# A matmul with batch normalisation: the weight blocks loaded by one GpSimd transfer each instead of four

## The chip, the cores and the metric

The kernel runs on one core of one Trainium2 chip. The metric is the device time of one execution in microseconds (us), without any profiler; before the change it is 207.76 us, the median of three runs (207.47 to 208.3). A profile is one separate execution of the same program, recorded by the hardware profiler. Engines are named as in the profile: PE multiplies matrices (PEld is its weight load), DVE and ACT are the vector and the scalar engine, POOL is GpSimd, SP is the engine that here only starts transfers. A core has 16 DMA engines, which carry out every transfer, whichever engine issues it.

## What is computed

```python
def reference(x, weight, gamma, beta, eps):     # x (16, 512, 1024), weight (1024, 768), float32
    y = np.matmul(x, weight)                    # (16, 512, 768)
    mean = np.mean(y, axis=(0, 1), keepdims=True)
    var = np.var(y, axis=(0, 1), keepdims=True)
    y_norm = (y - mean) / np.sqrt(var + eps)
    return (gamma * y_norm + beta).astype(np.float32)
```

The 16 x 512 rows are one long dimension of 8192. Every output column needs its mean and variance over all 8192 rows before its first value can be stored.

## The kernel before

**Tiling.** The 8192 rows are worked through in 16 chunks of 512 (`C`, `CH`); the first two chunks are loaded in halves of 256 rows (`QR`). The 768 output columns are six blocks of 128. The 1024 input columns (`k`) are the contracted dimension. They lie on the 128 partitions in an unusual order, which lets DVE transpose x in blocks of 32: `k = 256 i + 64 jw + 2 c + e`, with `i` from 0 to 3, `c` from 0 to 31, and the partition is `32 i + c`. What is left on each partition are four blocks `jw` with two neighbours `e` each. A product over all of k is thus eight matmuls (`jw`, `e`) that add up in PSUM.

**The weight.** `w_sb` holds it as bf16, `[128, 4 (jw), 2 (e), 768]`. Block `jw` of it is read from four separate pieces of DRAM, one for each `i`: 32 lots of two neighbouring rows, which lie one behind another (32 x 2 x 768 x 4 bytes = 197 KB), and the four pieces start 256 rows apart. The transfers are GpSimd's and turn float32 into bf16 on the way, so that 786 KB are read and 393 KB are written for a block. `load_w(jw, jw1)` (L378) issues one transfer for each `i`, to 32 partitions; it is called for block 0, for block 1, and for blocks 2 and 3 together, so there are 12 weight transfers.

**x.** `load_x` (L386) loads some rows with four GpSimd transfers in the same manner, one for each `i`, each to 32 partitions, into a piece of the buffer `ring`; 256 rows are 1.05 MB read and 0.52 MB written. DVE transposes what came (`turn_x`, L421 or L414) into `xT_sb`. For the first two pieces the transpose is in two halves, blocks 0 and 1 and then 2 and 3.

**How the first microseconds run.** The loads are put in the order (L426): x piece 0, w block 0, x piece 1, w block 1, w blocks 2 and 3, then the other x pieces. On PE come, in this order (L754 to 771):

- `wake(8)`, matmuls on a constant tile (L574, and 22 small ones, L577), whose result is not used;
- `part(0, 1, [0])`: x piece 0 times w block 0;
- `wake(2)` (`FILL`), the same unused work again;
- `part(1, 2, [0])`: x piece 1 times w block 0;
- `part(0, 2, [1])`: both pieces times w block 1;
- then the first chunk times w blocks 2 and 3, and after that chunk by chunk.

Products of the first two column blocks are `rows_unit` (L493, x is the stationary side), those of the other four are `col_unit` (L558).

**Who sets the order.** Nothing is issued as the Python text has it. Each piece of work is a `Task` with a due time (`prio`), a cost for each engine that may do it, and what it depends on. `arrange()` runs through them in modelled time and writes out a fixed order for every engine; `seq()` holds the engines to it. Transfers are modelled by `Wires`: a task's cost on its queue is the time that issuing takes, its `dma` the time on the wires, and `count` the number of its transfers. A queue has eight places for transfers under way (`LANES = 8`), and so it is in the program too: a ninth GpSimd transfer isn't issued before the first has landed, a tenth before the second has, and so on. The planner's figures for a weight task are L436 to 438:

```python
took = 4 * 192 * 4 * (n1[0] - n) / 4 * PER_KB * 1.024
w_ready[n] = task(t, {"POOL": (2.0, 2.0)}, load_w(n, *n1), dma=took)
w_ready[n].count = 4
```

`make_identity` is a small GpSimd task of its own (`idt`), due after the last weight block and put wherever GpSimd has room.

**After the loads.** Column sums and squares are gathered while the chunks go by (L642 to L698), then columns are normalised and stored, block by block, under the matmuls of the later blocks. The last block ends with the statistics, a normalisation by DVE (L1280), transposes by PE (L1028), copies by ACT (L1293) and the stores.

Of the kernel before, what the change touches and what calls it, by code (L numbers as in the profile page):

```python
# [227 lines left out]
def kernel(  # L228
# [9 lines left out]
    nc = tc.nc  # L238
# [52 lines left out]
    def seq(bi):  # L291

        ins = bi.ins
        prev = last.get(ins.engine)
        if prev is not None:
            tc.add_manual_dep(
                ins, prev,
                mybir.DependencyInfo(mybir.DependencyClass.NoSync, mybir.DependencyReason.DATA),
                reason="order",
            )  # L300
        last[ins.engine] = ins.name
        return bi
# [48 lines left out]
    def task(prio, engines, emit, deps=(), lock=False, **kw):  # L351
        t = Task(prio, engines, emit, deps, **kw)
        t.lock = lock
        tasks.append(t)
        return t

    def dve(occ):
        return {"DVE": (occ, occ + 0.09)}

    def act(occ):  # L360
        return {"ACT": (occ, occ + 0.11)}
# [14 lines left out]
    w_ready, x_ready, x_slot, plain, last_loads = {}, {}, {}, {}, []  # L376

    def load_w(jw, jw1):  # L378
        def emit(eng):
            rows = weight.rearrange("(i jw c e) n -> i c jw (e n)", i=4, jw=JW, e=2)  # L380
            dst = w_sb.rearrange("p jw e n -> p jw (e n)")
            for i in range(4):
                seq(nc.gpsimd.dma_start(dst[32 * i:32 * i + 32, jw:jw1], rows[i, :, jw:jw1]))
        return emit

    def load_x(m0, rows, slot):  # L386
        def emit(eng):
            x_bf = piece(slot).bitcast(bf16).rearrange("p (t k) -> p t k", k=KQ)
            slot.tile = x_bf
            src = x_flat[m0:m0 + rows].rearrange("(t r) k -> r t k", r=32)  # L390
            for i in range(4):
                bi = seq(nc.gpsimd.dma_start(x_bf[32 * i:32 * i + 32], src[:, :, KQ * i:KQ * (i + 1)]))  # L392
            slot.loader.ins = bi.ins
        return emit
# [8 lines left out]
    def turn_x(xslot, slot, m0, t0, jw0, jw1, new, rows=QR):  # L403
        def emit(eng):
            single = m0 // CH in SINGLE
            if new:
                xT_sb = xtpool.tile([P, JW, 2, CH] if single else [P, JW, CH, 2], bf16, tag="xT")
                slot.tile = xT_sb
            half, row = divmod((m0 + 32 * t0) % CH, QR)
            if single:  # L410
                src = xslot.tile[:, t0:t0 + rows // 32].rearrange("p t (jw c e) -> p t jw e c", jw=JW, e=2)
                dst = slot.tile[:, :, :, half * QR + row:half * QR + row + rows]
                dst = dst.rearrange("p jw e (t r) -> p t jw e r", r=32)
                seq(nc.vector.transpose(dst[:, :, jw0:jw1], src[:, :, jw0:jw1]))  # L414
                return
            src = xslot.tile[:, t0:t0 + rows // 32].rearrange("p t k -> p (t k)").bitcast(f32)
            src = src.rearrange("p (t jw c) -> p t jw c", jw=JW, c=32)
            dst = slot.tile.rearrange("p jw m e -> p (jw m e)").bitcast(f32)
            dst = dst.rearrange("p (jw q t r) -> p q t jw r", jw=JW, q=QPC, r=32)
            dst = dst[:, half, row // 32:(row + rows) // 32, jw0:jw1]  # L420
            seq(nc.vector.transpose(dst, src[:, :, jw0:jw1]))  # L421
        return emit
# [9 lines left out]
    t = 1.0  # L432
    affine = None
    for kind, n, *n1 in order:
        if kind == "w":
            took = 4 * 192 * 4 * (n1[0] - n) / 4 * PER_KB * 1.024  # L436
            w_ready[n] = task(t, {"POOL": (2.0, 2.0)}, load_w(n, *n1), dma=took)
            w_ready[n].count = 4
            t += 2.1 * (n1[0] - n)
            if n1[0] == JW:  # L440
                idt = task(t, {"POOL": (0.6, 0.6)}, lambda eng: make_identity(nc, ident))
                task(t, act(0.25), lambda eng: seq(nc.scalar.copy(ident32, ident)), [idt])
            continue
        rows = n1[0] if kind == "p" else QR if kind == "x" else CH
        m0 = n if kind == "p" else n * rows
        if m0 == M // 2:
            affine = task(t, {"SP": (5.0, 7.0)}, load_affine, [x_ready[m0 // CH - 3, 0, JW]])
        slot = Slot(rings, rows // 32 * KQ // 2)
        load = task(
            t, {"POOL": (2.68 * rows / CH, 2.68 * rows / CH)}, load_x(m0, rows, slot), dma=rows * K * 4 / 1024 * PER_KB * 1.024,  # L450
            takes=[slot])
        load.count = 4
        slot.loader = load
        last_loads.append(load)
        t += 2.7 * rows / QR
        for i in range(rows // QR):
            c, q = divmod(m0 // QR + i, QPC)
            for j0, j1 in ((0, JW // 2), (JW // 2, JW)) if m0 < CH else ((0, JW),):
                new = q == 0 and j0 == 0
                x_ready[c, q, j1] = task(  # L460
                    -1000 + t, dve((2.2 if c in SINGLE else 1.16) * (j1 - j0) / JW + 0.02),
                    turn_x(slot, x_slot[c], m0, i * QR // 32, j0, j1, new), [load],
                    uses=[slot] if new else [slot, x_slot[c]], takes=[x_slot[c]] if new else [])
                if not new:
                    x_ready[c, q, j1].deps.append(x_ready[c, 0, JW // 2 if m0 < CH else JW])
            x_ready.setdefault((c, q, JW // 2), x_ready[c, q, JW])
        if rows % QR:
            t0 = rows // QR * QR // 32
            m1 = m0 + 32 * t0
            c, q = divmod(m1 // QR, QPC)  # L470
            x_ready["tile", m1 // P] = task(
                -1000 + t, dve(0.63), turn_x(slot, x_slot[c], m0, t0, 0, JW, False, P),
                [load, x_ready[c, 0, JW]], uses=[slot, x_slot[c]])
            x_ready[c, q, JW] = x_ready[c, q, JW // 2] = x_ready["tile", m1 // P]
# [796 lines left out]
    for c, r0, rows in ends:  # L1271
        due = E + 2.0 + 0.6 * c
        n = max(rows // CH, 1)
# [70 lines left out]
```

## Time and profile before

| what | value |
|---|---|
| time, median of three runs | 207.76 us (207.47 to 208.3) |
| span of the profiled execution | 206.5 us |
| PE busy | 191.4 us, 93% of the span |
| DVE, ACT, POOL busy | 156.3, 139.8, 132.0 us |
| weight transfers issued by POOL (L383) | 12: eight of 96 KB, four of 192 KB written |
| their time on POOL, each | 492 to 537 ns, median 510 ns |
| x transfers issued by POOL (L392) | 76, median 644 ns on POOL |
| chain that ended last, share of PE | 82% |

The profiled execution's own time is its span of 206.5 us and what lies around it; the median of the unprofiled runs is 1.3 us above the span. In a row of the timeline the columns are the start in us from the span's start, the duration in us, the engine, the line of the kernel, the operation, output and input tiles, their shapes, and how many instructions of the kind are merged; behind it, in brackets, the idle time before it and what ended that. In a row of the windows, each engine's busy us in the window are followed by the granted PE clock (1.00 is full speed), the mean busy share of the DMA engines, and the GB/s that they moved. Bytes of a transfer are counted as written, so a weight or x transfer counts half of what it reads.

### The profile page before, as it was taken

To read this page: it belongs to the slowest core of one execution; us is meant where nothing else is said; L and a number is where in the kernel's file an instruction comes from. 1 tells how busy PE (TensorE), PEld (TensorE's weight loads), DVE (VectorE), ACT (ScalarE), POOL (GpSimd) and SP (SyncE) were. 2 spreads that over 40 slices of the span, in tenths; PEclk is the share of its full clock that TensorE was granted. 3 is DMA by queue.
4 is the path that set the end of the run, shared out by engine and by line. 5 is a ranking of instruction groups with operands and counts; after the bars stand their busy time and mean duration, and the time that the engine had idled before them with its cause. 6 is when DMAs were issued, how large, how long until landed. Compare 5 with 4: busy or idle time off the path is not lost.

```text
span 206.5 us, 3506 instructions
## 1 busy us (share of the span) xinstructions
PE 191.4 (93%) x1211; PEld 116.3 (56%) x1226; DVE 156.3 (76%) x238; ACT 139.8 (68%) x248; POOL 132.0 (64%) x148
## 2 busy tenths in 40 slices
PE   7998999999999999999999999999999999996900
PEld 3465564747488888777875444444444445553600
DVE  4220779999999999968989998977999648947900
ACT  2000560369989999998978767997376776866950
POOL 7877964877488999999304999599954440440000
PEclk9999999999999999999999999999999999999995
DMA  5999999999999999999676898999999999999898
GB/s 55 169 168 193 192 196 196 196 198 197 190 193 197 197 197 195 196 197 195 110 120 199 311 339 307 267 350 307 315 317 245 291 325 308 274 341 347 254 347 243
DMA packets 98497, 48.73 MB, mean 236 GB/s; under 512 B 24240, under 2 KB 97968, under 8 KB 98480
## 3 DMA queue, kind: packets, MB, share of 16 engines
q0 software_dynamic: 34688, 18.36, 65.1%
q1 hardware_dynamic: 63792, 30.16, 52.8%
q8 instruction: 9, 0.15, 0.3%
q14 instruction: 8, 0.07, 0.1%
HBM read 36.71 MB, written 25.17 MB: 300 GB/s over the span
## 4 chain that ended last, share of the span: by engine, by line
PE 82%; DMA 8%; ACT 3%; issue 1%; POOL 1%; DVE 1%; ACTq 0%; POOLq 0%
PE y_ps L558 51%; PE y_ps L493 23%; DMA ring<-in_x_dram 5%; PE y_ps L798 4%; ACT o_sb L1293 3%; DMA w_sb<-in_weight_dram 3%; PE o_ps L1028 2%; PE a_ps L887 1%; POOL ring L392 1%; PE y_ps L736 1%; PE o_ps L1058 0%; ACTq L1339 0%; PE tot_ps L855 0%; DVE fin L743 0%; ACT y_sb L746 0%
## 5 line engine op out<-in xcount | busy, mean ns | idle before, releaser
L558 PEld LDWEIGHTS <-w_sb 128*128 128x128 bf16 x512 | 49.7, 97 | 57.4
L558 PE MATMUL y_ps<-x_pl,w_sb 128*128 128x512 bf16 x256 | 60.5, 379 | 0.3
L392 POOL DMA_DIRECT2D ring<-in_x_dram x76 | 47.5, 630 | 13.0 <-DVE xT_sb L414 5.0
L558 PE MATMUL y_ps<-xT_sb,w_sb 128*128 128x512 bf16 (+1 forms) x241 | 55.1, 376 | 0.4
L493 PE MATMUL y_ps<-w_sb,xT_sb 128*128 128x256 bf16 x448 | 50.7, 273 | 0.6 <-DMA w_sb<-in_weight_dram 0.6
L493 PEld LDWEIGHTS <-xT_sb 128*128 128x128 bf16 x448 | 43.6, 98 | 8.3 <-issue 1.7
L421 DVE STREAM_TRANSPOSE xT_sb<-ring 128x1024 f32<-128x1024 f32 (+1 forms) x29 | 31.2, 1111 | 12.4 <-DMA ring<-in_x_dram 12.2
L694 DVE BATCH_NORM_STATS2 stats<-y_ps 128x6 f32<-128x512 f32 x46 | 30.9, 687 | 12.7 <-PE y_ps L558 12.5
L698 ACT CAST y_sb<-y_ps 128x512 bf16<-128x512 f32 x51 | 29.4, 590 | 14.5 <-DVE stats L694 12.4
L926 POOL TENSOR_TENSOR ring<-ring,sum 128x1024 f32<-128x1024 f32 (+1 forms) x11 | 23.7, 2193 | 14.6 <-DVE ring L921 14.5
L649 POOL TENSOR_TENSOR sum<-sum,sq_sb 128x512 f32<-128x512 f32 x21 | 26.9, 1281 | 3.2 <-ACT sq_sb L642 2.1
L642 ACT ACTIVATE sq_sb<-y_ps 128x512 f32<-128x512 f32 x28 | 16.3, 607 | 18.0 <-PE y_ps L493 17.1
L645 DVE TENSOR_TENSOR sum<-y_ps,sum 128x512 f32<-128x512 f32 x28 | 18.9, 675 | 9.1 <-ACT sq_sb L642 7.8
L530 ACT COPY x_pl<-xT_sb 128x1024 bf16<-128x1024 bf16 x24 | 24.4, 1052 | 1.7 <-DVE xT_sb L421 1.7
L655 ACT CAST y_sb<-y_ps 128x512 bf16<-128x512 f32 x28 | 16.0, 599 | 7.8 <-DVE sum L645 7.6
L530 POOL COPY x_pl<-xT_sb 128x1024 bf16<-128x1024 bf16 x15 | 16.1, 1108 | 8.0 <-DVE x_pl L530 5.2
L921 DVE TENSOR_TENSOR ring<-y_sb,a_ps 128x1024 f32<-128x1024 bf16 (+1 forms) x16 | 16.7, 1080 | 0.3 <-DMA out_dram<-ring 0.3
L1139 POOL TENSOR_TENSOR ring<-ring,sum 128x1024 f32<-128x1024 f32 x4 | 9.6, 2412 | 11.0 <-DVE ring L1135 11.0
L1193 ACT CAST ring<-ring 128x1024 f32<-128x1024 bf16 x15 | 15.7, 1049 | 1.0 <-DMA ring<-y_sb 1.0
L1028 PE MATMUL o_ps<-ident,y_sb 128*128 128x128 bf16 x104 | 14.2, 221 | 2.2 <-DVE y_sb L1280 2.0
L414 DVE STREAM_TRANSPOSE xT_sb<-ring 128x2048 bf16<-128x2048 bf16 x6 | 13.5, 2289 | 0.2 <-DMA ring<-in_x_dram 0.2
L574 PE MATMUL idle_ps<-idle_sb 128*128 128x512 f32 x20 | 11.2, 717 | 1.5 <-DVE idle_sb L314 1.5
(97 smaller groups left out, 155.0 us busy)
## 6 DMA issues: line engine op xcount, KB each, us to landing
out_dram<-ring SPq DMA_DIRECT2D x38, 512.0 KB, 3.7
ring<-in_x_dram POOLq DMA_DIRECT2D x52, 256.0 KB, 8.8
out_dram<-o_sb SPq DMA_DIRECT2D x6, 512.0 KB, 4.9
ring<-in_x_dram POOLq DMA_DIRECT2D x16, 128.0 KB, 5.3
out_dram<-ring SPq DMA_DIRECT2D x4, 256.0 KB, 3.0
w_sb<-in_weight_dram POOLq DMA_DIRECT2D x8, 96.0 KB, 5.1
w_sb<-in_weight_dram POOLq DMA_DIRECT2D x4, 192.0 KB, 5.9
ring<-in_x_dram POOLq DMA_DIRECT2D x4, 192.0 KB, 8.1
```

The source lines that it names most:

```text
L392: bi = seq(nc.gpsimd.dma_start(x_bf[32 * i:32 * i + 32], src[:, :, KQ * i:KQ * (i + 1)]))
L421: seq(nc.vector.transpose(dst, src[:, :, jw0:jw1]))
L493: seq(nc.tensor.matmul(y_ps[:, s], x_of(c, jw, e, t * P, (t + 1) * P), w_sb[:, jw, e, 0:NA], start=(s == 0 and jw == 0 and e == 0), stop=( ...
L530: seq(nc.scalar.copy(dst, pairs) if eng == "ACT" else ENG[eng].tensor_copy(dst, pairs))
L558: seq(nc.tensor.matmul(y_ps, w_sb[:, jw, e, nt * P:(nt + 1) * P], moving(c, jw, e, q0 * QR, q1 * QR, parted), start=(jw == 0 and e == 0 an ...
L645: seq(nc.vector.tensor_add(sum1, slot.tile[:, 0:n], sum1))
L649: seq(ENG[eng].tensor_add(acc, acc, state["sq"][:, 0:n]))
L694: seq(nc.vector.bn_stats(dst, slot.tile))
L698: seq(nc.scalar.copy(y(nt, c), slot.tile))
L921: seq(nc.vector.tensor_mul(slot.o, y_row[c].y[:, s0:s1], aff[0][:, None, :].to_broadcast([P, n, NA])))
L926: seq(ENG[eng].tensor_add(slot.o, slot.o, row[:, None, :].to_broadcast([P, n, NA])))
L1028: seq(nc.tensor.transpose(dst, src, ident))
```

## The change

Each weight block becomes one transfer over all 128 partitions. Its destination is `[128, 1536]`, its source the four pieces at once, `[4 (i), 32 (c), 1536 (e n)]`. The call for blocks 2 and 3 issues two such transfers, one for each block. The planner is told that a weight task takes GpSimd 0.6 us for each block where it was 2.0 us for a task, and that it is one transfer or two where it was four. The time on the wires is left as it was, and so are all due times and everything else.

```diff
         def emit(eng):
             rows = weight.rearrange("(i jw c e) n -> i c jw (e n)", i=4, jw=JW, e=2)
             dst = w_sb.rearrange("p jw e n -> p jw (e n)")
-            for i in range(4):
-                seq(nc.gpsimd.dma_start(dst[32 * i:32 * i + 32, jw:jw1], rows[i, :, jw:jw1]))
+            for j in range(jw, jw1):
+                seq(nc.gpsimd.dma_start(dst[:, j], rows[:, :, j]))
         return emit
...
             took = 4 * 192 * 4 * (n1[0] - n) / 4 * PER_KB * 1.024
-            w_ready[n] = task(t, {"POOL": (2.0, 2.0)}, load_w(n, *n1), dma=took)
-            w_ready[n].count = 4
+            w_ready[n] = task(t, {"POOL": (0.6 * (n1[0] - n), 0.6 * (n1[0] - n))}, load_w(n, *n1), dma=took)
+            w_ready[n].count = n1[0] - n
             t += 2.1 * (n1[0] - n)
```

## The prediction

> **What bounds the kernel now.** I read the waits of PE first, because PE is busy for 191.4 of 206.5 us. The rows give what was waited for, the us in total, how often, and the longest.
>
> ```profile
> PE o_ps L1028 <- DVE y_sb L1280: 2.0, 1, 2.0
> PE idle_ps L574 <- DVE idle_sb L314: 1.5, 1, 1.5
> PE y_ps L493 <- DMA w_sb<-in_weight_dram: 0.6, 1, 0.6
> ```
>
> That is all of it: a start, a wait of 0.6 us for the last weight blocks, and one wait at the end. Whatever delays PE early is therefore carried to the end, and whatever is loaded earlier than PE needs it gives nothing. Next, PE's timeline at the start:
>
> ```profile
> 10.67 1.39 PE L577 MATMUL idle_ps<-idle_sb 128*128 128x128 bf16 x22
> 11.89 0.60 PE L493 MATMUL y_ps<-w_sb,xT_sb 128*128 128x256 bf16 x4
> ...
> 14.96 0.60 PE L493 MATMUL y_ps<-w_sb,xT_sb 128*128 128x256 bf16 x4
> ...
> 17.40 1.74 PE L558 MATMUL y_ps<-xT_sb,w_sb 128*128 128x512 bf16 x7
> 19.74 1.91 PE L493 MATMUL y_ps<-w_sb,xT_sb 128*128 128x256 bf16 x16 [0.60 <-DMA w_sb<-in_weight_dram]
> ```
>
> The unused matmuls end at 12.06, and the first product of block 0 begins without any wait: block 0 has landed by then, though the trace doesn't say by how much. The second piece of x is used at 14.96, blocks 2 and 3 from 19.74. Then the rows of GpSimd, which issues the loads, and of DVE, which transposes x:
>
> ```profile
> 1.29 2.44 POOL L392 DMA_DIRECT2D ring<-in_x_dram  x4 [0.84 <-POOLq L1325]
> 3.73 1.99 POOL L383 DMA_DIRECT2D w_sb<-in_weight_dram  x4
> ...
> 8.49 1.31 DVE L421 STREAM_TRANSPOSE xT_sb<-ring 128x512 f32<-128x512 f32 x2 [5.36 <-DMA ring<-in_x_dram]
> 13.45 1.30 DVE L421 STREAM_TRANSPOSE xT_sb<-ring 128x512 f32<-128x512 f32 x2 [3.65 <-DMA ring<-in_x_dram]
> ```
>
> Last, windows, for what the wires carry (the last figure is GB/s, as written):
>
> ```profile
> 6.00:7.00 1.00, 1.00 (x4) 0.52 (x3) 0.00 (x0) 0.13 (x1) 0.92 (x3) 1.00 1.15 148
> ...
> 16.00:17.00 1.00, 1.00 (x12) 0.88 (x10) 0.00 (x0) 0.00 (x0) 0.96 (x2) 1.00 1.10 212
> 17.00:18.00 1.00, 0.94 (x7) 0.54 (x6) 0.00 (x0) 0.00 (x0) 0.60 (x2) 1.00 1.05 203
> ...
> 25.00:50.00 25.00, 24.88 (x161) 15.59 (x161) 22.59 (x25) 12.49 (x21) 16.98 (x24) 1.00 1.45 196
> ```
>
> The sixteen DMA engines together write about 200 GB/s, in the stretch of the weights (around 16 to 18) as in the steady one: 12.5 GB/s each.
>
> **The change part by part.**
>
> *Issuing.* Twelve weight issues of 0.51 us become four. A transfer of 128 lots lies between the rows of 32 lots (0.51) and of 256 (an x transfer of 128 KB, about 0.60); I take 0.55. GpSimd is spared 12 x 0.51 - 4 x 0.55 = 3.9 us, 1.4 of them ahead of x piece 1. With a place for eight transfers, x piece 1 gets its first three issues at 4.3 instead of 5.84, and its fourth waits for x's very first. None of this is on PE's path by itself: at most it ends the wait of 0.6 us.
>
> *Where a transfer's bytes go.* No GpSimd transfer of the trace has this shape: all 88 have 32 as their outer count on both sides, this one has 128 partitions on the one and four pieces on the other. So the price is bounded from both sides. If all sixteen engines share it, a block takes 0.393 MB / 200 GB/s = 2.0 us as now. If the four pieces are what is shared out, four engines write 98 KB each, at 12.5 GB/s 7.9 us. I take the second: four is the outer count of the source, and both sides can be cut alike by nothing larger without breaking a piece up. There is no nearer row, so both ends stay.
>
> [...] No run here shows a transfer on fewer than sixteen.
>
> *Block 0.* Adding up the windows from 2 us, 8 + 118 + 137 + 123 + 148 = 534 GB/s x us, so the 0.524 MB of x piece 0 are through at 6.9. Block 0, issued at 4.3, follows on its four engines: 6.9 + 7.9 = 14.8, and with 0.5 us from the last byte to the waiting engine (an estimate: x piece 0 is through at 6.9 by the sum and at 8.49 by DVE, with block 0 mixed in, so 0.3 to 1) it is there at 15.3. PE stands idle from 12.06 and begins its first product at 15.3 instead of 11.89: 3.4 us late. Bounds: if the four engines are free of x piece 0 at 5.9 and run at 13 GB/s (the row of 212), 13.8; if they are free at 8.5 and run at 12.2 (the row of 196), 17.1.
>
> *x piece 1* is queued behind block 0 on those four engines: 0.524 MB / 200 GB/s = 2.6 us more, to 17.4, landed at 17.9, half transposed (0.65) at 18.6. PE has by then done the first products and the unused work, 14.96 - 11.89 = 3.07 us, to 18.4. It waits 0.3 more and uses piece 1 at 18.7 instead of 14.96.
>
> *Blocks 1 to 3* go to the other engines after x piece 1, if each has four of its own: through x at 9.6 there, issued by 9.2 at the latest (the twelfth transfer waits for the fourth, landed by 8.49) and so begun by 11, 7.9 us: landed between 18.0 and 19.5. From piece 1 to the need of blocks 2 and 3 PE has 19.14 - 14.96 = 4.18 us of work, so that is at 22.9: no wait, and the old one of 0.6 us is gone. PE begins them at 22.9 instead of 19.74: **3.2 us late**.
>
> *Behind it.* The thirteenth transfer, x piece 2, now waits for block 0 (15.3; before, 14.67), and GpSimd's sums of squares stand behind it in its queue. The first of them ran at 23.27, and it shifts with PE by 3.2. The wires are full from 18 on with 0.4 MB of each piece less ahead of them, so pieces 2 and 3 land by 22 and 25, and DVE used them at 22.65 and 25.71 for a PE that is now 3.2 us later. That hides it; without the cover each us of lateness would be one of PE's. PE then has no wait to shrink until the end, and the end shifts with it.
>
> *The planner.* The order is written anew from changed figures. The early order of PE hangs on due times and stays; farther on, small exchanges can't win much (PE's only later wait is the 2.0 us at the end) and could lose some: -0.3 to +1.0, taken as 0.
>
> Sum: span 206.5 + 3.2 = 209.7; with 1.3 around it, **211.0 us**. Of the forecast alone: from block 0 at 13.8 (piece 1 used at 17.2, +1.6) to 17.1 (piece 1 at 20.7, +5.1) 209.3 to 212.9.
>
> **The rivals.**
>
> 1. *All sixteen engines share each transfer* (not slower): block 0 lands before 12.06, which is the point that decides; PE's start is as now, blocks 2 and 3 are in time, and the 0.6 us are gone: 207.76 - 0.6 = 207.2, or 206.9 to 208.2 with the planner. For it: today's transfers use the wires fully. Against it: the outer count of four. 12%.
> 2. *Four engines, and the same for every block.* Then three blocks of 7.9 us follow one another behind x piece 1 (17.4): the last is through at 41.1, in place of 19.6 today; PE waits until 41.6 instead of 19.74, 22 us: about 229.5. The trace speaks neither for nor against. 7%.
> 3. *Four engines, and PE's clock falls in the gap.* In the trace PE's last work is at 196.4, and the granted clock is still 1.00 at 199 to 200 and 0.76 from 200 to 201, so it fell some 4 us into idleness; my gap is 3.2 us. If it falls, the 1.35 us of first products and 1.7 of unused work take twice as long; less the 0.3 that piece 1 is waited for, +2.8: 213.8. 6%.
>
> **How the numbers follow.** The forecast has 75%. The range is 208.8 to 213.9: the forecast's own with the planner's bounds, and rival 3; it leaves out rivals 1 and 2 (19%). What a measurement of this kernel can tell from no change is about 0.5%, 1.0 us. Faster: 3%, a lucky order under rival 1. Same: 10%, most of rival 1 and the low edge of the forecast. Slower: 87%.
>
> **What would show it.** Four weight issues on GpSimd near 0.55 us; issue to landing of block 0 about 11 us where it was 5.1; a wait of PE for `w_sb` of about 3 us at 12, in place of the 0.6 at 19; first products at 15.3, piece 1 at 18.7, blocks 2 and 3 at 22.9; GB/s falling while four engines alone are busy; after that the same PE rows, 3.2 us later. If block 0 lands in 5 us, the shape doesn't limit the engines and the forecast is wrong at its root; if PE waits again after 20, the blocks share engines.

## The result, and the profile after

The changed kernel takes 216.72 us (median of six runs, 213.81 to 218.25) where the kernel before takes 208.04 beside it (207.47 to 208.91): slower. Three of the six runs lie more than 1.5% above the fastest and are set apart as slow; without them the ratio is 1.0335, with a 95% interval of 1.029 to 1.038, which is about 7 us. The forecast was 211.0 with a range of 208.8 to 213.9: the right direction and, as the runs below show, the right cause, but less than half of the size. The profiled execution, with a span of 216.4 us, is the longest of the six; a second one, told of below, has 213.3.

The waits of PE in the changed kernel (what was waited for, us in total, times, longest):

```profile
PE y_ps L493 <- DMA w_sb<-in_weight_dram: 6.6, 1, 6.6
PE o_ps L1028 <- DVE y_sb L1280: 2.0, 1, 2.0
PE idle_ps L574 <- DVE idle_sb L314: 1.5, 1, 1.5
PE y_ps L493 <- DVE xT_sb L421: 1.2, 1, 1.2
```

The wait of 0.6 us is gone; in its place stand 6.6 us for block 0 and 1.2 for x piece 1. The two other rows are as before. PE's timeline shows where they lie:

```profile
18.92 1.01 PE L493 MATMUL y_ps<-w_sb,xT_sb 128*128 128x256 bf16 x4 [6.55 <-DMA w_sb<-in_weight_dram]
19.73 1.92 PE L558 MATMUL y_ps<-xT_sb,w_sb 128*128 128x256 bf16 x8
21.44 2.98 PE L574 MATMUL idle_ps<-idle_sb 128*128 128x512 f32 x4
25.65 0.61 PE L493 MATMUL y_ps<-w_sb,xT_sb 128*128 128x256 bf16 x4 [1.23 <-DVE xT_sb L421]
...
29.69 1.91 PE L493 MATMUL y_ps<-w_sb,xT_sb 128*128 128x256 bf16 x16
```

Blocks 2 and 3 begin at 29.69, 9.95 us later than before, and the span is 9.9 us longer: all of the loss has been made by then, and PE carries it to the end, as forecast. The first products take 1.92 us for what took 1.07, so PE's clock has fallen. The windows of this kernel (the last three figures are the granted clock, the DMA share and GB/s) show it, and something else:

```profile
12.00:13.00 1.00, 0.37 (x7) 0.25 (x5) 0.00 (x0) 0.00 (x0) 0.00 (x0) 1.00 1.23 166
13.00:14.00 1.00, 0.00 (x0) 0.00 (x0) 0.00 (x0) 0.00 (x0) 0.00 (x0) 1.00 1.15 123
14.00:15.00 1.00, 0.00 (x0) 0.00 (x0) 0.00 (x0) 0.00 (x0) 0.00 (x0) 1.00 1.32 144
15.00:16.00 1.00, 0.00 (x0) 0.00 (x0) 0.00 (x0) 0.00 (x0) 0.00 (x0) 1.00 1.06 123
16.00:17.00 1.00, 0.00 (x0) 0.00 (x0) 0.00 (x0) 0.00 (x0) 0.00 (x0) 0.92 1.33 128
17.00:18.00 1.00, 0.00 (x0) 0.00 (x0) 0.00 (x0) 0.00 (x0) 0.00 (x0) 0.50 1.45 138
```

The clock is granted in full until nearly 17 and then halves. And the wires, which in this stretch have all four weight blocks to carry, move 123 to 144 GB/s where they moved about 200 before. GpSimd's timeline, and from the page the row of the weight transfers (count, KB each, us from issue to landing) and that of the software queue (packets, MB, share):

```profile
3.73 0.71 POOL L383 DMA_DIRECT2D w_sb<-in_weight_dram  x1
4.44 2.28 POOL L392 DMA_DIRECT2D ring<-in_x_dram  x4
...
19.17 0.60 POOL L392 DMA_DIRECT2D ring<-in_x_dram  x1 [9.55 <-DMA w_sb<-in_weight_dram]
```

```profile
q0 software_dynamic: 36096, 18.36, 67.4%
...
w_sb<-in_weight_dram POOLq DMA_DIRECT2D x4, 384.0 KB, 17.5
```

Four issues of 0.7 us, a landing after 17.5 us (the median of the four) where it was 5 to 6, and 1,408 packets more than the 34,688 of before although there are eight transfers fewer. The trace also holds sixteen completions for each transfer: of those of block 0, twelve come between 6.8 and 7.8 us and four between 17.4 and 18.9.

The written order of PE, DVE, ACT and SP is the same in both kernels, instruction by instruction. On GpSimd only the weight transfers and the place of the identity beside them differ. So the planner's new figures changed nothing behind the loads.

### The profile page after: what moved, and what is told of

It is laid out like the page before. It is cut to its first block, busy times and chain, and to the rows that moved or that the text cites. A ratio compares the mean times of both kernels' runs of the same rounds, so it can differ in the third digit from the quotient of the medians.

```text
span 216.4 us, 3494 instructions
## 1 busy us (share of the span) xinstructions
PE 194.2 (90%) x1211; PEld 119.1 (55%) x1226; DVE 156.6 (72%) x238; ACT 139.2 (64%) x248; POOL 129.7 (60%) x140
## 3 DMA queue, kind: packets, MB, share of 16 engines
q0 software_dynamic: 36096, 18.36, 67.4%
## 4 chain that ended last, share of the span: by engine, by line
PE 81%; DMA 9%; ACT 3%; POOL 2%; DVE 1%; issue 1%; ACTq 0%; POOLq 0%
PE y_ps L558 50%; PE y_ps L493 22%; DMA ring<-in_x_dram 9%; PE y_ps L798 3%; ACT o_sb L1293 2%; PE o_ps L1028 2%; POOL ring L392 2%; PE a_ps L887 1%; PE y_ps L736 1%; PE o_ps L1058 0%; ACTq L1339 0%; PE tot_ps L855 0%; DVE xT_sb L421 0%; POOL w_sb L383 0%; DVE fin L743 0%
## 5 line engine op out<-in xcount | busy, mean ns | idle before, releaser
L558 PE MATMUL y_ps<-xT_sb,w_sb 128*128 128x512 bf16 (+1 forms) x241 | 56.0, 381 | 0.4
L698 ACT CAST y_sb<-y_ps 128x512 bf16<-128x512 f32 x51 | 29.0, 590 | 12.5 <-DVE stats L694 11.5
L642 ACT ACTIVATE sq_sb<-y_ps 128x512 f32<-128x512 f32 x28 | 16.9, 617 | 30.0 <-PE y_ps L493 29.7
L649 POOL TENSOR_TENSOR sum<-sum,sq_sb 128x512 f32<-128x512 f32 x21 | 27.6, 1316 | 8.8 <-ACT sq_sb L642 8.1
L645 DVE TENSOR_TENSOR sum<-y_ps,sum 128x512 f32<-128x512 f32 x28 | 18.9, 674 | 7.6 <-ACT sq_sb L642 6.4
L655 ACT CAST y_sb<-y_ps 128x512 bf16<-128x512 f32 x28 | 15.6, 611 | 7.1 <-DVE sum L645 7.0
L574 PE MATMUL idle_ps<-idle_sb 128*128 128x512 f32 x20 | 12.6, 795 | 1.5 <-DVE idle_sb L314 1.5
## 6 DMA issues: line engine op xcount, KB each, us to landing
w_sb<-in_weight_dram POOLq DMA_DIRECT2D x4, 384.0 KB, 17.5
```

Source lines behind the costliest of these rows:

```text
L558: seq(nc.tensor.matmul(y_ps, w_sb[:, jw, e, nt * P:(nt + 1) * P], moving(c, jw, e, q0 * QR, q1 * QR, parted), start=(jw == 0 and e == 0 an ...
L642: seq(nc.scalar.activation(sq_sb[:, 0:n], slot.tile[:, 0:n], AF.Square))
L645: seq(nc.vector.tensor_add(sum1, slot.tile[:, 0:n], sum1))
L649: seq(ENG[eng].tensor_add(acc, acc, state["sq"][:, 0:n]))
L698: seq(nc.scalar.copy(y(nt, c), slot.tile))
```

## The experiments

Theory A is that of the forecast: a transfer is shared out by its outer count, four here, so four engines carry each block; added to it, once the profile was seen, is that the groups slow each other down. The edits are shown against the changed kernel, and in all runs the written orders of PE, DVE, ACT and SP stay as they are, but for the longer warm-up of one and the last run, where it is said.

**The planner's figures alone.**

```diff
-            for j in range(jw, jw1):
-                seq(nc.gpsimd.dma_start(dst[:, j], rows[:, :, j]))
+            for i in range(4):
+                seq(nc.gpsimd.dma_start(dst[32 * i:32 * i + 32, jw:jw1], rows[i, :, jw:jw1]))
```

> The planner's new figures with the old twelve weight transfers: the instructions of PE, DVE, ACT and SP stand in the same order as before, and on GpSimd only x piece 1 is moved ahead of the identity. If the loss is made by the new transfers' shape (theory A), the time is that of before, 208.0 within 0.7. If it is made by the order that the planner writes (rival P), it is that of the changed kernel, 214 to 218.

Measured: 209.15 us beside 208.28 for before, a ratio of 1.0039 (1.0005 to 1.0074). That is a little above the expected 208.0 within 0.7. PE's wait for blocks 2 and 3 is 1.1 us here instead of 0.6. The order of the loads costs about 0.8 us (0.1 to 1.5 by the interval), a small part of the loss; rival P falls.

**One transfer with an outer count of 128.**

```diff
-            rows = weight.rearrange("(i jw c e) n -> i c jw (e n)", i=4, jw=JW, e=2)
+            rows = weight.rearrange("(jw p e) n -> p jw (e n)", jw=JW, e=2)
...
-                seq(nc.gpsimd.dma_start(dst[:, j], rows[:, :, j]))
+                seq(nc.gpsimd.dma_start(dst[:, j], rows[:, j]))
```

> One transfer a block over 128 partitions, as in the change, but its source is 128 lots that lie one behind another (other rows of w than the reference takes, so the products differ): the outer count is 128 on both sides. Theory A (four engines because the outer count of the source is 4): sixteen engines share it, block 0 lands before 12, PE has no wait but that at the end, 207.0 to 208.2, and the number of 4-byte packets is below that of before, not above. Rival B (a single large transfer lands late, however it is shared out): block 0 lands after 15 and the time is over 211.

Measured: 207.88 us, a ratio of 0.9971 (0.9943 to 1.0). The same number of transfers, of the same size, to the same 128 partitions. The waits of PE, and the queue's row of the page:

```profile
PE o_ps L1028 <- DVE y_sb L1280: 2.0, 1, 2.0
PE idle_ps L574 <- DVE idle_sb L314: 1.5, 1, 1.5
```

```profile
q0 software_dynamic: 34560, 18.36, 65.0%
```

No wait for a weight is left: the 0.6 us that rival 1 of the prediction spoke of are gone, in a run that takes other rows of w than the reference. What makes the loss is the source with its four pieces, not the large transfer; rival B falls. The packets can be counted: 32,768 of x, 512 lots of w and 16 for each of 80 transfers are 34,560. The changed kernel has 36,096, 384 more for each of its four weight transfers, which is 12 x 32: by this count the twelve engines that carry none of a block get 32 empty packets each, as many as each of the other four has lots. (A lot is one packet here, 512 of 3,072 bytes in the traces of both kernels, and the empty ones are the 4-byte packets of the expectations: 1,408 on this queue before, 2,816 in the changed kernel. The trace doesn't name a packet's engine.)

**Block 0 alone as one transfer.**

```diff
-            for j in range(jw, jw1):
-                seq(nc.gpsimd.dma_start(dst[:, j], rows[:, :, j]))
+            for to, of in [(dst[:, j], rows[:, :, j]) for j in range(jw, jw1)] if jw == 0 else [(dst[32 * i:32 * i + 32, jw:jw1], rows[i, :, jw:jw1]) for i in range(4)]:
+                seq(nc.gpsimd.dma_start(to, of))
```

The planner's cost and count are those of each form, here and in the next run.

> Only block 0 is one transfer; blocks 1 to 3 are four each, spread as before. Theory A with contention (block 0 was slow from 11.5 us on only because the three other blocks' groups of engines ran beside it): block 0 lands at about 15.4, PE begins its first product at 15.5 and not at 18.9, x piece 1 is used near 18.7, blocks 2 and 3 near 23 to 24.5, time 211 to 213. Rival C (block 0's shape is slow by itself): first product near 18.9 again, time 214 to 218.

Measured: 214.2 us, a ratio of 1.0254 (1.0178 to 1.033), span 212.8. Its windows, and its PE timeline:

```profile
13.00:14.00 1.00, 0.00 (x0) 0.00 (x0) 0.00 (x0) 0.00 (x0) 0.00 (x0) 1.00 0.30 58
14.00:15.00 1.00, 0.00 (x0) 0.00 (x0) 0.00 (x0) 0.00 (x0) 0.00 (x0) 0.95 0.26 52
15.00:16.00 1.00, 0.00 (x0) 0.00 (x0) 0.00 (x0) 0.00 (x0) 0.00 (x0) 0.50 0.31 45
```

```profile
16.17 1.01 PE L493 MATMUL y_ps<-w_sb,xT_sb 128*128 128x256 bf16 x4 [4.76 <-DMA w_sb<-in_weight_dram]
...
18.69 3.39 PE L574 MATMUL idle_ps<-idle_sb 128*128 128x512 f32 x4
21.92 0.60 PE L493 MATMUL y_ps<-w_sb,xT_sb 128*128 128x256 bf16 x4
...
25.95 1.25 PE L493 MATMUL y_ps<-w_sb,xT_sb 128*128 128x256 bf16 x10
```

From 13 to 16 block 0 is nearly alone on the wires, and they carry about 50 GB/s: a quarter of 200, four engines of sixteen. The first product is at 16.17 and not at 18.9: block 0 isn't slow by itself, and rival C falls. But the expected time was missed from above: from first product to piece 1 PE took 5.75 us for what takes 3.07. It did not wait for piece 1 in that time, which had reached DVE 2.7 us behind block 0, as the prediction has it:

```profile
18.86 1.30 DVE L421 STREAM_TRANSPOSE xT_sb<-ring 128x512 f32<-128x512 f32 x2 [8.71 <-DMA ring<-in_x_dram]
```

What it lost it lost by the clock, which fell in the gap of 4.76 us.

**Block 0 as four, the others as one each.**

```diff
-            for j in range(jw, jw1):
-                seq(nc.gpsimd.dma_start(dst[:, j], rows[:, :, j]))
+            for to, of in [(dst[32 * i:32 * i + 32, jw:jw1], rows[i, :, jw:jw1]) for i in range(4)] if jw == 0 else [(dst[:, j], rows[:, :, j]) for j in range(jw, jw1)]:
+                seq(nc.gpsimd.dma_start(to, of))
```

> Block 0 is four transfers as before; blocks 1 to 3 are one each. Theory A with contention: first product at 11.9, x piece 1 used at 15 as before, then PE waits for block 1, which begins near 10 to 11 on four engines and takes 12 us beside blocks 2 and 3: landed near 23, PE's wait 6 to 8 us at 16.3, its clock falls in it, time 214 to 218. Without contention (each packet at 248 ns) block 1 lands near 19.5, the wait is 3 us and the time 210.5 to 211.5. If block 0 alone were the cause (rival D), 207.5 to 208.5.

Measured: 216.16 us, a ratio of 1.0344 (1.0277 to 1.041). First product at 12.47; the waits of PE begin with

```profile
PE y_ps L493 <- DMA w_sb<-in_weight_dram: 6.1, 1, 6.1
```

which ends at 23.14, when block 1 is there: near 23, as expected with contention, and not near 19.5. The groups do slow each other down, and block 0 isn't the only cause (rival D falls): either half of the change costs about what the whole costs, because in the whole PE waits for block 0 while the others land.

**The clock.** The run with block 0 alone as one transfer, with more small unused matmuls.

```diff
-    SMALL = 22
+    SMALL = 100
```

> As the run with block 0 alone as one transfer, with 100 small unused matmuls in place of 22, which keep PE at work until about 16.4, when block 0 lands. If the fall of the clock in PE's wait cost there what the rows say (first products and unused work at half speed), PE uses x piece 1 at 19 to 19.6 where it was 21.9, and the time is 2 to 3 us below that run, 211 to 212.3. If the clock cost nothing because PE had to wait for data anyhow, the time is that run's, 214.2.

Measured: 214.64 us (213.26 to 217.57, a ratio of 1.0313, 1.0274 to 1.0352): no gain over 214.2. PE's timeline, of the longest execution:

```profile
19.85 0.61 PE L493 MATMUL y_ps<-w_sb,xT_sb 128*128 128x256 bf16 x4
...
26.33 3.06 PE L493 MATMUL y_ps<-w_sb,xT_sb 128*128 128x256 bf16 x16 [2.29 <-DMA w_sb<-in_weight_dram]
```

Piece 1 is used 2.1 us earlier, as expected of a kept clock. Then PE waits 2.29 us for blocks 2 and 3, whose transfers had to wait for one of the eight places until block 0 landed (GpSimd stood idle for 7.92 us before it issued the next at 16.63), and begins them at 26.33, not before the 25.95 of the run without. In that run, too, the last of these blocks had landed only at 25.3, by the completions in its trace, so that an earlier piece 1 could have gained no more than 0.7 us there. The saving at piece 1 is real in this execution, and the next bound eats it up; the shorter executions have no profile.

**Why the groups are slow: places in DRAM.** In the changed kernel the sixteen strips start at multiples of 196,608 bytes.

```diff
+            lots = weight.rearrange("(l e) n -> l (e n)", e=2)
...
-                seq(nc.gpsimd.dma_start(dst[:, j], rows[:, :, j]))
+                seq(nc.gpsimd.dma_start(dst[:, j], lots[124 * j:124 * j + 132].rearrange("(i c) n -> i c n", c=33)[:, 0:32]))
```

> As the changed kernel, all four blocks one transfer each with an outer count of 4 in the source, but the sixteen strips start at other places of w (33 lots apart within a block, 124 between blocks, where they were 128 and 32), so other rows of w are taken than the reference takes. If the weight transfers slow each other down because their strips lie at multiples of 196,608 bytes in DRAM (theory M): the windows around 13 to 16 us show 190 to 200 GB/s and not 120 to 145, block 0 lands near 15.5, the blocks 1 to 3 near 20, time 210.5 to 213. If the slowness comes from elsewhere (rival S, the writes to the same partitions): windows, landings and time as in the changed kernel, 214 to 218.

Measured: 215.2 us, a ratio of 1.0329 (1.03 to 1.0357), and in the windows 154, 184 and 163 GB/s from 13 to 16, block 0 at 16.9. Faster windows than those shown of the changed kernel, but its second profile below has the same: theory M isn't borne out.

**Or partitions.** In all four transfers the four strips begin at partitions 0, 32, 64 and 96. If each engine takes a strip and goes up it lot by lot, which is an assumption, as the traces hold no addresses, engines of several blocks write to the same partition at about the same time.

```diff
+            for j, s in [(j, 16 * max(j - 1, 0)) for j in range(jw, jw1)]:
+                [seq(nc.gpsimd.dma_start(dst[lo:hi, j], of)) for lo, hi, of in ((0, s, rows[0, 0:s, j]), (s, P, rows[:, 0:32 - s // 4, j])) if lo < hi]
```

> As the changed kernel, but blocks 2 and 3 go to the partitions from 16 and from 32 on with four strips of 28 and of 24 lots, and what is left of each goes by a transfer of its own to the first 16 or 32 partitions (w isn't in the order of the reference there). The strips start in DRAM where those of the changed kernel do. If the slowness comes from several engines writing to the same partitions at the same time (rival S): the windows around 13 to 16 us show over 180 GB/s and block 0 lands near 15.5. If it comes from the places in DRAM (theory M): 120 to 150 GB/s there as in the changed kernel, block 0 after 17.5, time 213 to 218.

Measured: 214.21 us, a ratio of 1.0283 (1.025 to 1.0315), 152 to 163 GB/s, first product at 15.96. The run doesn't decide: its small transfers took the places of the large one of block 3, so three groups ran until 16 and not four, and twelve engines at 12.5 GB/s make 150. The three that follow compare four groups with four:

**The changed kernel again, and both shifts with four groups.** In the second and third the large transfers are issued ahead of the small ones, so that the small ones are issued only after 16 us; the third has the strips of the DRAM run as well. The fence behind the expectations is the second's, without the lines that it replaces.

> The changed kernel itself once more, as the base for the two runs beside it on one chip: windows around 13 to 16 us at 120 to 165 GB/s, block 0 landed between 16.5 and 19, time 213.5 to 217.5. If the slow windows of its first profile were an accident of that execution, these show 190 or more and block 0 lands before 16.

> As the run with the shifted partitions, but the two large transfers of blocks 2 and 3 are issued ahead of the two small ones, so that all four groups of engines run side by side as in the changed kernel. If writes to the same partitions make the slowness (rival S): over 180 GB/s around 13 to 15 us, block 0 lands near 15.5 to 16. If the earlier run was fast only because it had three groups and not four: 120 to 165 GB/s, block 0 near 17 to 19.

> Partitions shifted as in the run beside it and the strips in DRAM as in the run with other distances. If both places matter, sixteen engines at the rate of one alone: 190 to 200 GB/s around 13 to 15 us, block 0 near 15.4. If only the partitions matter, as the run beside it within 10 GB/s; if neither does, 120 to 165 GB/s.

```diff
+            cut = [(j, 16 * max(j - 1, 0)) for j in range(jw, jw1)]
+            parts = [(s, P, j, rows[:, 0:32 - s // 4, j]) for j, s in cut] + [(0, s, j, rows[0, 0:s, j]) for j, s in cut if s]
+            for lo, hi, j, of in parts: seq(nc.gpsimd.dma_start(dst[lo:hi, j], of))
```

Their windows from 13 to 15, first the changed kernel's, then with the partitions shifted, then with both:

```profile
13.00:14.00 1.00, 0.00 (x0) 0.00 (x0) 0.00 (x0) 0.00 (x0) 0.00 (x0) 1.00 1.13 154
14.00:15.00 1.00, 0.00 (x0) 0.00 (x0) 0.00 (x0) 0.00 (x0) 0.00 (x0) 1.00 1.21 175
```

```profile
13.00:14.00 1.00, 0.00 (x0) 0.00 (x0) 0.00 (x0) 0.00 (x0) 0.00 (x0) 1.00 1.13 209
14.00:15.00 1.00, 0.00 (x0) 0.00 (x0) 0.00 (x0) 0.00 (x0) 0.00 (x0) 1.00 1.11 212
```

```profile
13.00:14.00 1.00, 0.00 (x0) 0.00 (x0) 0.00 (x0) 0.00 (x0) 0.00 (x0) 1.00 1.04 200
14.00:15.00 1.00, 0.00 (x0) 0.00 (x0) 0.00 (x0) 0.00 (x0) 0.00 (x0) 1.00 1.13 203
```

| | time, us | ratio (95%) | first product | piece 1 used | blocks 2, 3 begun |
|---|---|---|---|---|---|
| changed kernel again | 215.3 | 1.0347 (1.0302 to 1.0392) | 17.21 | 22.82 | 26.86 |
| partitions shifted | 214.39 | 1.029 (1.0254 to 1.0325) | 16.13 | 21.95 | 25.98 |
| both shifted | 213.78 | 1.0265 (1.0234 to 1.0297) | 16.95 | 21.56 | 25.58 |

With other partitions for two blocks the sixteen engines are back at the full 200 GB/s; other places in DRAM add nothing to it. The packets say the same. From 13 to 16 us a lot took its engine 444 and 344 ns on average in the two profiles of the changed kernel and 347 with other places in DRAM, but 259 and 266 in the two runs with shifted partitions and 248 with block 0 alone. So the slowness goes with the partitions that the blocks are written to: rival S, shown by one profile of each run. That several engines are at the same place at the same time remains the author's reading of it. Whether such a place is a single partition or something wider isn't told apart: the shifted transfers also have their four strips 28 or 24 partitions apart instead of 32, and blocks 0 and 1 still share their places. Block 0 itself is there at 16.1 and 17.0, the second time later than the 15.4 expected. What remains, 5.3 to 5.9 us over before (213.78 and 214.39 less 208.51), is the cost of four engines at about their full rate, of x piece 1, which reached DVE 3.6 to 4.1 us behind block 0 (20.50 and 20.18), and of the fall of the clock.

Of the changed kernel's second profile, the rows of PE and DVE that the table and the next section rest on:

```profile
17.21 1.01 PE L493 MATMUL y_ps<-w_sb,xT_sb 128*128 128x256 bf16 x4 [5.04 <-DMA w_sb<-in_weight_dram]
22.05 1.30 DVE L421 STREAM_TRANSPOSE xT_sb<-ring 128x512 f32<-128x512 f32 x2 [12.06 <-DMA ring<-in_x_dram]
22.82 0.61 PE L493 MATMUL y_ps<-w_sb,xT_sb 128*128 128x256 bf16 x4 [1.16 <-DVE xT_sb L421]
```

**Two transfers with an outer count of two.** For block 0, with the other blocks as four each.

```diff
+            for to, of in [(dst[64 * h:64 * h + 64, 0], rows[2 * h:2 * h + 2, :, 0]) for h in range(2)] if jw == 0 else ...
...
+    MODE = {2:'pe',3:'pe',4:'pe'}
+    RAW, RAWADD, RAWDUE = {}, ...
```

> Block 0 as two transfers over 64 partitions each, with an outer count of 2 in the source; blocks 1 to 3 as four each. The transposes after the loads are PE's here and not the DMA's, so only the first 30 us are compared, not the time. If the outer count sets the number of engines (theory A), two engines carry each half: again 32 lots an engine, block 0 lands near 16, PE's first product there, as with one transfer; where block 0 is alone on the wires about 49 GB/s; the software queue has 35,024 + 16 + 2 x 14 x 32 - 12 x 32 = 35,552 packets. If the loss came with the size of a transfer or with 128 partitions (rival B), half the size lands by 12 to 13.

Measured: first product at 16.19, after 16.17 with one transfer, and 43 to 55 GB/s while block 0 is alone. From its page:

```profile
q0 software_dynamic: 35552, 18.36, 61.0%
```

That is the expected number to the packet: two engines for each half. Half the size brought nothing here, where the outer count halved with it.

## Why the prediction was wrong in its size, and what in it was right

That four engines carry a block, and that PE carries an early delay to the end, was right. What failed is the size, in two terms of the sum. In the second profile blocks 2 and 3 begin 7.1 us late and not 3.2.

- *"... four engines write 98 KB each, at 12.5 GB/s 7.9 us"*: this holds for one block alone. With all four under way a lot took 444 and 344 ns in the first and second profile instead of 248, and block 0 was there at 18.9 and 17.2, not at 15.3.
- *From block 0 to the use of x piece 1*, 15.3 to 18.7 or 3.4 us in the sum: 6.7 and 5.6 us were measured, because piece 1 reached DVE 6.0 and 4.8 us behind block 0 and not 2.6. Where it came after 2.7, with block 0 alone, the way took 5.75 us all the same, by the clock. The sum put the clock at nothing because "my gap is 3.2 us". Yet its own late bound, block 0 at 17.1, makes a gap of 5.0 us, and it had seen the clock fall after some 4.

| step | before | forecast | block 0 alone as one | changed, second profile | changed, first profile |
|---|---|---|---|---|---|
| first product | 11.89 | 15.3 | 16.17 | 17.21 | 18.92 |
| x piece 1 used | 14.96 | 18.7 | 21.92 | 22.82 | 25.65 |
| blocks 2 and 3 begun | 19.74 | 22.9 | 25.95 | 26.86 | 29.69 |
| span | 206.5 | 209.7 | 212.8 | 213.3 | 216.4 |

*What bounds the kernel.* Right: what PE loses before 30 us it loses for good. The late start of blocks 2 and 3 (9.95 and 7.12 us in the two profiles) is the loss in span (9.9 and 6.8), and behind it PE has no wait that it didn't have before.

*Issuing.* Mis-sized, without effect: 0.70 us an issue, not 0.55, the "rows of 32 lots (0.51) and of 256" being no bound for it.

*Where a transfer's bytes go.* Right: four engines, shown by the run with 128 as its outer count (no wait for a weight), by a quarter of the wires' rate (45 to 58 GB/s with block 0 nearly alone), by four late completions of sixteen, and by the packets: the counts of 384 and 448 empty packets a transfer, for outer counts of four and two, are 12 x 32 and 14 x 32. The choice of four was the author's estimate; no trace of before shows it. One transfer a block over 128 partitions took 207.88 us with 128 as the source's outer count and 216.72 with four.

*"Block 0 ... is there at 15.3."* 0.9 early where block 0 is the only such transfer (16.17), and 1.9 to 3.6 in the changed kernel, where the second profile's 17.2 lies just past the late bound of 17.1. The rate was read from rows in which every transfer had 32 as its outer count. With all blocks under way, their strips starting at the same four partitions, the wires gave 123 to 144 GB/s in one profile and 154 to 175 in the other. That the groups would slow each other down was in no rival.

*"x piece 1 is queued behind block 0 on those four engines."* Right in kind, and the last bound in the changed kernel: DVE gets it at 24.88 in the first profile, 0.5 us after the work that would have hidden it has ended (24.42), and PE goes on at 25.65. Forecast was "landed at 17.9", 2.6 us behind block 0. It came 6.0 us behind it in the first profile (24.88 after 18.92) and 4.8 in the second (22.05 after 17.21); by their completions the fourth of its transfers came 3.1 and 2.6 us after the third. With block 0 alone it came 0.7 after it, so the delay goes with the other blocks' being single transfers too; how they make it isn't shown.

*"If each has four of its own."* Right, though no run on record before showed it; rival 2, the same four engines for every block, did not come: block 0 alone gives 50 GB/s, the four together two and a half to three and a half times that (123 to 175) and, with the partitions apart, four times. Blocks 1 to 3 landed at 25.6 to 26.2 in the first profile and at 22.4 to 23.1 in the second, by their completions, not "between 18.0 and 19.5", but still before PE came to them. The sign "if PE waits again after 20, the blocks share engines" misled: PE did wait again (1.2 us, to 25.65 and 22.82), for x piece 1.

*The gap and the clock.* "My gap is 3.2 us" was wrong with the step before, and with it the 6% of rival 3. The gap was 5.0 to 6.6 us, and the clock fell 4.5 and 4.3 us after PE's last work in the two profiles, 3.5 with block 0 alone. With other places in DRAM it fell after 4.8, though PE had been at work again for 0.5 us by then. Its price of "+2.8" was close: 5.75 us from first product to piece 1 with block 0 alone, against 3.37 (16.48 to 19.85) in the run that kept the clock, is 2.4. In the changed kernel, though, PE waits 1.2 us for piece 1 after it, so that the clock isn't what ends last there; and where it was kept, the next transfer took its place. What sets the 3.5 to 4.8 us isn't shown.

*The planner.* Bounded at -0.3 to +1.0, measured 1.0039 of 208.3, 0.8 us, with the old transfers.

*Range and level.* 209.3 less 0.3 is 209.0 and not 208.8, and rival 3 went into the range at its bare 213.8, without a late block 0 and without the planner. The 1.3 us "around" the span set the median of some runs against the profile of one; each run's own time lies 1.8 to 1.9 us above its span. That moves the level and not the difference.

*Rival 1* was wrong as a forecast of this change and right as a price: with sixteen engines the single transfers gain 0.4 us (207.88 against 208.28 beside it, 0 to 1.2 by the interval); its price said 0.6 us.

No version that computes the reference beat the kernel before. One with eight weight transfers, each with an outer count of 32, has no measurement.

## What to carry to other kernels

Before two transfers are made one, write down the outer count of both sides as they will be issued: a gather of four pieces into 128 partitions has four on the source side, and here only four of sixteen engines carried it, by the sum 8 us for what took 2, and with block 0 alone measured at 12.4 us from issue to landing for what took 5.1. Then look which partitions the transfers under way write to, not only how many engines there are: here four transfers to the same partitions moved 123 to 175 GB/s, where one alone moved about 50. And price a wait of PE together with the clock that it may lose, and the relief from it together with the bound that comes next.

## What the runs showed of the hardware that wasn't expected

- A GpSimd transfer that four engines carried had 384 4-byte packets more than the sixteen of every other, 12 x 32, and two that two engines carried had 896, 2 x 14 x 32: by this count an engine that has no part in a transfer gets as many as a carrying engine has lots. The runs with shifted partitions fit too: 35,984 packets, with 28 and 24 lots an engine for two of the blocks.
- Four weight transfers under way to the same partitions moved 123 to 175 GB/s as written, against 200 to 212 with two blocks' partitions shifted by 16 and 32. How much of it comes from the very same partition and how much from its neighbours isn't shown.
- How strongly the weight transfers hold each other up differs between two executions of the same changed kernel, 444 ns a lot against 344. What sets it isn't shown.
